# Transformer layer on one core: where sums of w_out, the SSM's preparation and the first transposes stand in the engines' order

## The chip, the cores and the metric

The kernel runs on one core of one Trainium2 chip. The metric is the time of one execution on the device in microseconds (us), lower is better.

## What is computed

One layer of a decoder, in fp32, for one sequence of T = 1024 tokens with D = 1024 (from the reference):

```
x <- LN1(alpha*x + 1/2 * SwiGLU_1(x))                      first FFN ("f1"), FF = 2816
[z_a | z_u | z_v | g_a | g_b] = x @ W_in                   one combined input projection
y_a = S5(z_a) -> GLU -> @ U_a                              diagonal complex SSM branch (causal scan)
y_b = gMLP chunked causal spatial gating(z_u, z_v) -> @ U_b
x <- LN2(alpha*x + (sig(g_a)*y_a + sig(g_b)*y_b) @ W_out)
x <- LN3(alpha*x + 1/2 * SwiGLU_2(x))                      second FFN ("f2")
x <- x + sig(x @ W_pg) * (p @ W_pp)

SwiGLU(x): h = x @ w_in; gate, up = split(h); (silu(gate) * up) @ w_out
```

## The kernel before

Every fp32 product runs on TensorE (PE) as three fp32r matmuls (hi*hi, hi*lo, lo*hi). `split` (L81, L82) makes the two parts: ScalarE (ACT) casts the high part, VectorE (DVE) subtracts it for the low part.

**FFN, into the hidden layer.** `hidden` goes over 22 chunks of 128 hidden columns with gate and up together, by Strassen's scheme in Winograd's form: 7 products per chunk (`prod`, 12 matmuls each) instead of 8. The operands from x are seven blocks, B11, B21, B22, T1 to T4; those from the weights are made per chunk by `pair_steps`: sums s12 and s34 (L312 to L318, DVE), then four splits, named wha/wla, whs/wls, wht/wlt, wh4/wl4 in the trace. The products land in PSUM banks and are read into e0 to e3 by ACT copies (L595, L597, L599, L606) and DVE additions (L603, L608, L610), with ACT's Silu (L604, L609) and the gate (L612, L617) between them. The trace prints e0 to e3 as e_f. ACT and DVE run their instructions in one order each, so L606 stands behind L604, which needs L603. After an odd chunk, `total` (L576) makes sums of two chunks' G, and `put` (L573) stores them from the POOL queue.

**FFN, out of it.** This is Strassen's scheme too, and needs differences of rows of w_out. For each of 11 pairs in each FFN a job "wload" (L256) fetches two blocks of rows of 512 KB on SP's queue, and a job "wsum" (L248) makes four subtracts of 128x512 on DVE and two stores (L250) on POOL's queue. The tiles come from the pool that `phase["rows"]` names: five buffers with tag "s", which s12 and s34 use too, in the first FFN; three buffers with tag "y" in the second. Raw weights have three buffers, split ones five.

**Pre jobs.** At chunks 8 and 14 of the first FFN, jobs "pre" make the split weights of the second FFN's first two chunks and store them; they are loaded back at its start (L241).

**Start.** `x_T` (L763 to L768) transposes a block of x on PE into a transpose bank (`tbank`, two of them) and splits it into xc. Fourteen of these steps are the `feed` of the first chunk, which runs as two halves (columns 0 to 256 and the rest) of seven products: one step ahead of the loop, then one before each product. In the first half a step is x_T of block 1 and a step of the weights' preparation; in the second, x_T of blocks 2 and 3. `turn_vecs` (L365, vecs_t) transposes the vectors of the layer, through the same kind of bank.

**SSM.** `xg_T` (L931 to L936) transposes z_a on PE and copies it, alternately on DVE and ACT, into xg. Then 8 slices follow: each prepares rotation powers (the "e-chain" on DVE, seven levels of L1397 to L1402 behind a copy L1459, and products on POOL and ACT), runs `states` (with a scan) and `outputs` (L1505, matmuls that read ssm_h). `defer(us, ...)` puts a step off by so much estimated PE time.

**Who sets the order.** PE's order is written by hand. On DVE, ACT, POOL and SP a scheduler sets it, except at the very start, where it is the order of the text. `tc.issue_after(i)` obliges it to put instructions behind i on the same engine, without a wait on a semaphore. The first instructions of an SSM slice are put behind the instructions recorded in `last` in this way.

Of the kernel before, what the change touches and what calls it, by code (L numbers as in the profile page):

```python
# [13 lines left out]
ALU = mybir.AluOpType  # L14
# [3 lines left out]
P = 128  # L18
# [12 lines left out]
NCK = T // QS  # L31
# [27 lines left out]
def hybrid_layer(ctx, tc, t, out):  # L59
    nc = tc.nc  # L60
# [157 lines left out]
                i += n  # L218
            g_loaded[ji] = g

    n_made, on_chip, w_rows = [0], {}, {}

    def make_jobs(upto, loading=True):
        while n_made[0] <= min(upto, len(jobs) - 1):
# [6 lines left out]
            if kind in ("pair", "pre"):  # L231
                bs = pair_tiles(i, phase["pre" if kind == "pre" else "pair"][1])
                if raws:
                    for _ in pair_steps(i, loaded[li], loaded[li + 1], bs):
                        pass
                for b, d in zip(bs, pre_d[key[-1]] if kind == "pre" or not raws else ()):
                    for x in range(2):
                        if kind == "pre":
                            nc.gpsimd.dma_start(out=d[x], in_=b[x].bitcast(F32))
                        else:  # L240
                            nc.sync.dma_start(out=b[x].bitcast(F32), in_=d[x])  # L241
                made[key] = pair_views(bs)
            elif kind == "wsum":

                ws = w_rows.pop(key[::2])
                (b11, b12), (b21, b22) = ((r[:, :512], r[:, 512:]) for r in ws)
                for o, x, y in ((b11, b12, b11), (b12, b22, b12), (b22, b22, b11), (b21, b21, b22)):
                    DVE.tensor_tensor(out=o, in0=x, in1=y, op=ALU.subtract)  # L248
                for y in range(2):
                    nc.gpsimd.dma_start(out=wt_d[key[0]][key[2]][y], in_=ws[y])  # L250
            elif kind == "wload":
                p, tag = phase["rows"]
                ws = w_rows[key[::2]] = [p.tile([P, 1024], F32, name=f"wo_{key[0]}_{key[2]}_{y}", tag=tag) for y in range(2)]
                for y in range(2):
                    f = 2 * key[2] + y
                    nc.sync.dma_start(out=ws[y], in_={"f1": w1o, "f2": w2o}[key[0]][f * P:(f + 1) * P, :])  # L256
            else:
                for j in range(i, min(i + RAWBUFS, len(jobs))):
                    load_g(j)
                w, (o_nm, f) = None, (key[0], key[-1])  # L260
                if raws or kind == "out" and order_of(key).index(f) >= WBUFS:
                    w = (wsp_p.tile([P, 1024], F32R, name=f"wh{i}", tag="hi"),
                         wsp_p.tile([P, 1024], F32R, name=f"wl{i}", tag="lo"))
                    on_chip[o_nm, f] = w
                made[key] = on_chip[o_nm, f]
                if raws:
                    split(*w, loaded[li])
                    if o_nm == "mo":
                        for x in range(2):
                            nc.gpsimd.dma_start(out=mo_d[f][x], in_=w[x].bitcast(F32))  # L270
                elif w:
                    for x in range(2):
                        nc.sync.dma_start(out=w[x].bitcast(F32), in_=mo_d[f][x])
                if kind == "out":
                    load_g(i)
                    g, ph = g_loaded.pop(i), phase[key[0]]
                    gh = ph["ghl"].tile([P, 3 * P], F32R, name=f"gh{i}", tag="gh")
                    gl = ph["ghl"].tile([P, 3 * P], F32R, name=f"gl{i}", tag="gl")
                    n = len(ph["sweeps"][key[2]]) * P
                    split(gh[:, :n], gl[:, :n], g[:, :n])  # L280
                    made[key] += (gh, gl)
# [277 lines left out]
    def hidden(nm, xc, g_d, ep, cut, feed=()):  # L559
# [3 lines left out]


        feed = list(feed)
        if feed:
            feed.pop(0)()
        for f, cs in [(0, slice(0, cut)), (0, slice(cut, HT))] + [(f, slice(0, HT)) for f in range(1, NF)]:
            if cs.start == 0:
                w, es = take((nm, "h", f), 0), [ep.tile([P, HT], F32, name=f"e{b}_{nm}_{f}", tag=f"e{b}",  # L570
# [2 lines left out]
                nc.gpsimd.dma_start(out=g_d[f // 2][x], in_=g)  # L573

            def total(x, o, a, b, op):
                DVE.tensor_tensor(out=o, in0=a, in1=b, op=op)  # L576
                put(x, o)

            b1, b2, b3 = (bank(f"p{b}_{nm}_{f}_{cs.start}") for b in range(3))
# [156 lines left out]
    with pool("xc1", side="right") as xc_p, ExitStack() as hs:  # L736
# [23 lines left out]
                    "T3": t13[:, hi], "T4": t24[:, hi]}, todo  # L760

        def x_T(j, name):
            tb, src = tbank(f"xt_x0_{j}_{name}"), blocks[j][name]  # L763
            for i in range(4):
                PE.transpose(tb[:, i * P:(i + 1) * P], src[:, i * P:(i + 1) * P], ident)
            cs = slice(j * P, (j + 1) * P)
# [6 lines left out]
        use = ("B11", "T1", "T2", "B21", "T3", "B22", "T4")  # L773
        for tt in (0, 4):
            load_x(tt)
        load_raws(1)
        for tt in (1, 5):
            load_x(tt)
        rows = load_vecs(ep)
        warm = const.tile([P, 1], F32, name="warm")  # L780
        ACT.activation(out=warm, in_=ident[:, 0:1], func=AF.Silu)
# [87 lines left out]
    with ExitStack() as mx:  # L869
# [62 lines left out]
        def xg_T(q):  # L932
            tb = tbank(f"xg_{q}")
            for i in range(4):
                PE.transpose(tb[:, i * P:(i + 1) * P], za[:, 4 * q + i, :, :].rearrange("p s i -> p (s i)"), ident)
            (ACT.copy if q % 2 else DVE.tensor_copy)(out=xg[:, 4 * q:4 * q + 4, :], in_=tb.rearrange("p (g c) -> p g c", c=NCK))  # L936

        for q in range(NG // 4):
            defer(3.0 + 1.3 * q, ("xg", q), lambda q=q: xg_T(q))
# [429 lines left out]
def ssm_slices(nc, sp, bank, tbank, par, ident, xg, y, defer, need):  # L1369
# [18 lines left out]
    for sl in range(NG // SG):  # L1388
# [80 lines left out]
        def states(sl=sl, t0=t0, tmp=tmp, e=e, er=er, ei=ei, x1=x1, x2=x2):  # L1469
# [23 lines left out]
            for ri, (p1, p2, op) in enumerate(((fr, fi, ALU.subtract), (fi, fr, ALU.add))):  # L1493
                DVE.tensor_tensor(out=y1, in0=gr, in1=p1, op=ALU.mult)
                DVE.tensor_tensor(out=y2, in0=gi, in1=p2, op=ALU.mult)
                for a in range(2):
                    hp = slice(a * NS, (a + 1) * NS)
                    DVE.tensor_tensor(out=hm[ri * NS:(ri + 1) * NS, :, a, 1:P], in0=y1[hp], in1=y2[hp], op=op)
            defer(10.0, ("ssm", sl), lambda: outputs(hm))

        def outputs(hm, sl=sl):
            py = bank(f"ssm_y_{sl}")
# [40 lines left out]
```

## Time and profile before

| | |
|---|---|
| median of 3 runs | 2087.19 us (2085.76 to 2092.68) |
| the profiled execution | 2087.66 us |
| its span, first to last instruction | 2086.0 us |
| mean granted clock of PE | 0.987 |
| PE busy | 2023.9 us, 97% |
| DVE, ACT, POOL busy | 64%, 38%, 14% |
| weight loads of the FFNs (L202) | 88 of 512 KB, median 4.5 us to landing |
| loads of w_out rows (L256) | 44 of 512 KB, median 5.2 us |

An engine's share is over the whole span; the costs of a reordering are read from the stretch in which it works. A granted clock of 1.00 is 2.4 GHz; the other level is 1.2 GHz, and a stretch's figure is a mean.

### The profile page before, as it was taken

The page shows a single profiled execution, that of the slowest core. Times are in us where ns is not written, and L with a number is a line of the kernel's source. Part 1 is how long each engine was busy: PE and PEld are TensorE (multiplying, and loading weights), DVE is VectorE, ACT ScalarE, POOL GpSimd, SP SyncE. Part 2 cuts the span into 40 slices and gives each one's busy share as a digit, 9 for nine tenths or more (in the row PEclk, how much of TensorE's full clock was granted, in tenths as well). Part 3 has the DMA queues.
Part 4 walks back from the last instruction along what each step waited for, and adds up shares of the span by engine and source line. Part 5 has one row for each costly group of instructions (what it writes and reads, how often), then busy time and mean ns, then how long its engine had stood idle before and what let it go on. Part 6 is the DMA issues. An engine that isn't in the chain of part 4 may idle for free.

```text
span 2086.0 us, 25640 instructions
## 1 busy us (share of the span) xinstructions
PE 2023.9 (97%) x9207; PEld 1673.7 (80%) x9207; DVE 1342.8 (64%) x2385; ACT 784.1 (38%) x1227; POOL 282.2 (14%) x443
## 2 busy tenths in 40 slices
PE   7999999999999998999999999889999999999999
PEld 7887878888888896788888788667888888788887
DVE  6767657668557673699544458666665655766852
ACT  4333333333335512334541136223333333334540
POOL 3102111110000132334021200111010010000000
PEclk9999999999999999999999999999999999999999
DMA  4537465547666461222316967883233236766411
GB/s 152 178 127 263 149 220 180 191 121 260 214 196 219 137 198 58 73 82 72 98 60 230 303 234 272 287 277 126 86 111 106 92 116 213 245 196 202 148 61 41
DMA packets 241887, 344.01 MB, mean 165 GB/s; under 512 B 21940, under 2 KB 145936, under 8 KB 241760
## 3 DMA queue, kind: packets, MB, share of 16 engines
q1 hardware_dynamic: 203248, 221.43, 33.7%
q0 software_dynamic: 31600, 108.37, 14.3%
q10 hardware_dynamic: 6912, 12.59, 1.6%
q8 instruction: 72, 1.18, 0.2%
q14 instruction: 55, 0.45, 0.1%
HBM read 232.60 MB, written 108.53 MB: 164 GB/s over the span
## 4 chain that ended last, share of the span: by engine, by line
PE 56%; issue 26%; DVE 7%; DMA 6%; POOL 3%; ACT 1%; SPq 0%; POOLq 0%; DVEq 0%; ACTq 0%
PE po_f L699 19%; PE p_f L555 15%; PE ppg L516 1%; PE ppg L517 1%; PE ppg L518 1%; DMA wo_f<-in_ffn_w_out_dram 1%; POOL g_f_S L573 1%; PE pgb L516 1%; PE pgb L517 1%; PE pgb L518 1%; PE po_mo L516 1%; PE pga L516 1%; PE po_mo L518 1%; PE po_mo L517 1%; PE pga L518 1%
## 5 line engine op out<-in xcount | busy, mean ns | idle before, releaser
L82 DVE TENSOR_TENSOR wl<-wr,wh 128x1024 fp32r<-128x1024 f32 (+1 forms) x254 | 288.0, 1140 | 193.9 <-ACT wh L81 177.6
L81 ACT CAST wh<-wr 128x1024 fp32r<-128x1024 f32 (+1 forms) x254 | 246.7, 978 | 433.3 <-PE po_f L699 153.5
L699 PE MATMUL po_f<-wh 128*128 128x512 f32 x616 | 243.1, 395 | 4.2 <-DVE xa L705 4.2
L699 PE MATMUL po_f<-wh,wl 128*128 128x512 f32 x616 | 241.0, 391 | 0.0
L699 PE MATMUL po_f<-wl,wh 128*128 128x512 f32 x616 | 240.9, 391 | 0.0
L699 PEld LDWEIGHTS po_f<-wh 128*128 128x128 f32 x616 | 116.4, 189 | 28.2 <-issue 4.5
L699 PEld LDWEIGHTS po_f<-wh,wl 128*128 128x128 f32 x616 | 116.3, 189 | 24.7
L699 PEld LDWEIGHTS po_f<-wl,wh 128*128 128x128 f32 x616 | 116.5, 189 | 23.6
L573 POOL DMA_DIRECT2D g_f_A<-e_f x66 | 36.0, 545 | 540.1 <-DVE e_f L612 273.8
L312 DVE TENSOR_TENSOR s<-wr 128x512 f32<-128x512 f32 x44 | 30.9, 702 | 119.6 <-DMA wr<-in_ffn_w_in_dram 119.6
L555 PE MATMUL p_f<-T4h,wh 128*128 128x512 f32 (+3 forms) x184 | 74.7, 406 | 15.1 <-ACT e_f L606 15.1
L555 PE MATMUL p_f<-T2h,whs 128*128 128x512 f32 (+3 forms) x184 | 72.0, 391 | 6.9 <-ACT e_f L595 6.9
L81 ACT CAST whs<-s 128x1024 fp32r<-128x1024 f32 x44 | 46.2, 1050 | 81.5 <-PE p_f L555 60.5
L555 PE MATMUL p_f<-T3h,wht 128*128 128x512 f32 (+3 forms) x184 | 72.2, 392 | 4.5 <-ACT e_f L599 4.5
L555 PE MATMUL p_f<-T4l,wh 128*128 128x512 f32 (+3 forms) x184 | 73.7, 400 | 0.4 <-DVE T4l L82 0.4
L555 PE MATMUL p_f<-T4h,wl 128*128 128x512 f32 (+3 forms) x184 | 73.5, 399 | 0.0
L555 PE MATMUL p_f<-T3l,wht 128*128 128x512 f32 (+3 forms) x184 | 71.3, 387 | 1.9 <-DVE T3l L82 1.9
L82 DVE TENSOR_TENSOR wlt<-s,wht 128x1024 fp32r<-128x1024 f32 x44 | 53.8, 1223 | 29.6 <-ACT wht L81 26.8
L81 ACT CAST wht<-s 128x1024 fp32r<-128x1024 f32 x44 | 46.2, 1049 | 70.9 <-PE p_f L555 70.6
L555 PE MATMUL p_f<-B11l,wha 128*128 128x512 f32 (+3 forms) x184 | 70.6, 384 | 1.7 <-DVE B11l L82 1.7
L555 PE MATMUL p_f<-T1h,whs 128*128 128x512 f32 (+3 forms) x184 | 71.0, 386 | 0.9 <-ACT whs L81 0.9
L555 PE MATMUL p_f<-T1h,wls 128*128 128x512 f32 (+3 forms) x184 | 70.9, 385 | 0.8 <-DVE wls L82 0.8
(391 smaller groups left out, 5225.6 us busy)
## 6 DMA issues: line engine op xcount, KB each, us to landing
wr<-in_ffn_w_in_dram SPq DMA_DIRECT2D x88, 512.0 KB, 4.5
wo_f<-in_ffn_w_out_dram SPq DMA_DIRECT2D x44, 512.0 KB, 5.2
wt_f<-wo_f POOLq DMA_DIRECT2D x44, 512.0 KB, 4.3
wr<-wt_f SPq DMA_DIRECT2D x88, 256.0 KB, 3.3
wr<-g_f_S SPq DMA_DIRECT2D x88, 256.0 KB, 3.7
g_f_A<-e_f POOLq DMA_DIRECT2D x66, 256.0 KB, 3.0
g_f_S<-g_f POOLq DMA_DIRECT2D x66, 256.0 KB, 4.4
wr<-in_ffn_w_out_dram SPq DMA_DIRECT2D x66, 256.0 KB, 3.5
```

Source lines behind the costliest of these rows:

```text
L81: ACT.copy(out=hi, in_=src)
L82: DVE.tensor_sub(out=lo, in0=src, in1=hi.bitcast(F32))
L312: DVE.tensor_tensor(out=s1, in0=a21, in1=a22, op=ALU.add)
L516: PE.matmul(acc, lhsT=ah, rhs=bh, start=start, stop=False)
L517: PE.matmul(acc, lhsT=ah, rhs=bl, start=False, stop=False)
L518: PE.matmul(acc, lhsT=al, rhs=bh, start=False, stop=stop)
L555: PE.matmul(acc[:, cs], lhsT=p, rhs=q, start=start and k == 0 and i == 0, stop=stop and k == HK - 1 and i == 2, skip_group_check=True)
L573: nc.gpsimd.dma_start(out=g_d[f // 2][x], in_=g)
L699: PE.matmul(acc[t], lhsT=a[:, c], rhs=b[:, :512], start=not more and i == 0 and k == 0, stop=i == NP - 1 and k == 2, skip_group_check=True)
```

## The change

Nothing is computed otherwise. (1) The four subtracts of a "wsum" are put behind the last `total` made so far on DVE, the two loads of a "wload" behind the last weight load on SP. (2) Two steps of the feed run ahead of the first chunk's loop instead of one. (3) Block 3's transposes use the product banks (`bank`, six) instead of the transpose banks. (4) x blocks 1 and 5 are loaded before the first weights. (5) The copies to xg are recorded in `last[0]` and `last[1]`, so that the preparation of the first slice stands behind them on DVE and ACT. (6) A slice's outputs are put off by 12.5 instead of 10.0.

```diff
-    n_made, on_chip, w_rows = [0], {}, {}
+    n_made, on_chip, w_rows, last_sum = [0], {}, {}, [None]
...
-                for o, x, y in ((b11, b12, b11), (b12, b22, b12), (b22, b22, b11), (b21, b21, b22)):
-                    DVE.tensor_tensor(out=o, in0=x, in1=y, op=ALU.subtract)
+                with tc.issue_after(last_sum[0].ins):
+                    for o, x, y in ((b11, b12, b11), (b12, b22, b12), (b22, b22, b11), (b21, b21, b22)):
+                        DVE.tensor_tensor(out=o, in0=x, in1=y, op=ALU.subtract)
...
-                for y in range(2):
-                    f = 2 * key[2] + y
-                    nc.sync.dma_start(out=ws[y], in_={"f1": w1o, "f2": w2o}[key[0]][f * P:(f + 1) * P, :])
+                with tc.issue_after(last_load[0].ins):
+                    for y in range(2):
+                        f = 2 * key[2] + y
+                        nc.sync.dma_start(out=ws[y], in_={"f1": w1o, "f2": w2o}[key[0]][f * P:(f + 1) * P, :])
...
-        if feed:
-            feed.pop(0)()
+        for fn in feed[:2]:
+            fn()
+        feed = feed[2:]
...
-                DVE.tensor_tensor(out=o, in0=a, in1=b, op=op)
+                last_sum[0] = DVE.tensor_tensor(out=o, in0=a, in1=b, op=op)
...
-            tb, src = tbank(f"xt_x0_{j}_{name}"), blocks[j][name]
+            tb, src = (bank if j == 3 else tbank)(f"xt_x0_{j}_{name}"), blocks[j][name]
...
-        load_raws(1)
         for tt in (1, 5):
             load_x(tt)
+        load_raws(1)
...
-            (ACT.copy if q % 2 else DVE.tensor_copy)(out=xg[:, 4 * q:4 * q + 4, :], in_=tb.rearrange("p (g c) -> p g c", c=NCK))
+            last[q % 2] = (ACT.copy if q % 2 else DVE.tensor_copy)(out=xg[:, 4 * q:4 * q + 4, :], in_=tb.rearrange("p (g c) -> p g c", c=NCK))
...
-            defer(10.0, ("ssm", sl), lambda: outputs(hm))
+            defer(12.5, ("ssm", sl), lambda: outputs(hm))
```

The line numbers of the rows below are those of the kernel they are taken from; the changed kernel's are one to three higher (L248 is L249, L256 is L258, L576 is L579, L603 is L606, L936 is L939).

DVE in chunk 1 of the second FFN, before. wo_f2_2_1 is the second row block of w_out's pair 2, wlt188 and wla190 are split weights, e0_f2_1 is chunk 1's e0:

```order
L248 TENSOR_TENSOR wo_f2_2_1_11838<-wo_f2_2_1_11838 128x512
L248 TENSOR_TENSOR wo_f2_3_0_12116<-wo_f2_3_0_12116 128x512
L82 TENSOR_TENSOR wlt188_11288<-s34_188_11292,wht188_11287 128x1024
L248 TENSOR_TENSOR wo_f2_3_0_12116<-wo_f2_3_1_12117,wo_f2_3_0_12116 128x512
L603 TENSOR_TENSOR e0_f2_1_11272<-e0_f2_1_11272,p1_f2_1_0_11277 128x512
```

And after the change, from the last sums of G of chunk 1 to L606 (the former L603) of chunk 2:

```order
L579 TENSOR_TENSOR g_f2_1_11410<-e0_f2_1_11272,g_f2_0_11269 128x512
L249 TENSOR_TENSOR wo_f2_0_0_11279<-wo_f2_0_0_11279 128x512
L249 TENSOR_TENSOR wo_f2_0_0_11279<-wo_f2_0_1_11280,wo_f2_0_0_11279 128x512
L249 TENSOR_TENSOR wo_f2_0_1_11280<-wo_f2_0_1_11280,wo_f2_0_0_11279 128x512
L314 TENSOR_TENSOR s12_192_11570<-wr176_11448 128x512
L249 TENSOR_TENSOR wo_f2_0_1_11280<-wo_f2_0_1_11280 128x512
L315 TENSOR_TENSOR s12_192_11570<-s12_192_11570,wr175_11307 128x512
L319 TENSOR_TENSOR s34_192_11571<-wr175_11307,wr176_11448 128x512
L320 TENSOR_TENSOR s34_192_11571<-wr175_11307,s12_192_11570 128x512
L82 TENSOR_TENSOR wlt190_11431<-s34_190_11435,wht190_11430 128x1024
L606 TENSOR_TENSOR e0_f2_2_11413<-e0_f2_2_11413,p1_f2_2_0_11418 128x512
```

Before, pair 3's subtracts stood ahead of chunk 1's L603; now pair 0's stand behind chunk 1's sums of G, with no subtract of a later pair before chunk 3's end.

SP's queue at the start of the second FFN, before:

```order
L256 DMA wo_f2_1_1_11559<-in_ffn2_w_out_dram 128x1024
L256 DMA wo_f2_2_0_11837<-in_ffn2_w_out_dram 128x1024
L202 DMA wr174_11305<-in_ffn2_w_in_dram 128x8x128
L256 DMA wo_f2_2_1_11838<-in_ffn2_w_out_dram 128x1024
L241 DMA wh4_186_11163<-pre1_3_0_286 128x512
L241 DMA wl4_186_11164<-pre1_3_1_287 128x512
L256 DMA wo_f2_3_0_12116<-in_ffn2_w_out_dram 128x1024
L256 DMA wo_f2_3_1_12117<-in_ffn2_w_out_dram 128x1024
L256 DMA wo_f2_4_0_12395<-in_ffn2_w_out_dram 128x1024
L202 DMA wr175_11307<-in_ffn2_w_in_dram 128x8x128
```

And after the change:

```order
L202 DMA wr174_11305<-in_ffn2_w_in_dram 128x8x128
L241 DMA wh4_186_11163<-pre1_3_0_286 128x512
L241 DMA wl4_186_11164<-pre1_3_1_287 128x512
L202 DMA wr175_11307<-in_ffn2_w_in_dram 128x8x128
L202 DMA wr176_11448<-in_ffn2_w_in_dram 128x8x128
L202 DMA wr177_11450<-in_ffn2_w_in_dram 128x8x128
L258 DMA wo_f2_1_0_11558<-in_ffn2_w_out_dram 128x1024
L258 DMA wo_f2_1_1_11559<-in_ffn2_w_out_dram 128x1024
L202 DMA wr178_11584<-in_ffn2_w_in_dram 128x8x128
```

The loads of w_out rows (wo) stood between the first weight loads (wr); now one pair's two follow four weight loads.

DVE at xg, after the change (before, all of the e-chain stood ahead of the first copy to xg):

```order
L82 TENSOR_TENSOR wl135_6626<-wr137_6381,wh135_6625 128x1024
L939 COPY xg_6617<-xg_0_6670 128x512
L939 COPY xg_6617<-xg_2_6694 128x512
L939 COPY xg_6617<-xg_4_6735 128x512
L939 COPY xg_6617<-xg_6_6759 128x512
L1462 COPY ssm_e_0_7014<-par_rot_4462 128x2 x2
L1400 TENSOR_TENSOR ssm_x1_0_7015<-ssm_e_0_7014,par_rot_4462 128x2
```

The copies have moved ahead of the whole e-chain, which begins with L1462.

## Rows read from the trace of the kernel before

**Rows 1.** The head of the page and its part 1, whole span
```profile
span 2086.0 us, 25640 instructions
PE 2023.9 (97%) x9207; PEld 1673.7 (80%) x9207; DVE 1342.8 (64%) x2385; ACT 784.1 (38%) x1227; POOL 282.2 (14%) x443
```

**Rows 2.** Table by stretches: stretch, its length, busy us (instructions) per engine, PEclk, DMA share, GB/s
```profile
18.00:60.00 42.00, 33.60 (x249) 31.83 (x247) 32.70 (x48) 21.84 (x40) 11.12 (x8) 0.92 0.21 65
60.00:100.00 40.00, 40.00 (x176) 32.69 (x175) 30.83 (x45) 15.72 (x22) 6.35 (x12) 1.00 0.57 191
160.00:200.00 40.00, 36.92 (x160) 29.50 (x159) 26.88 (x38) 16.89 (x24) 7.43 (x14) 1.00 0.76 262
280.00:320.00 40.00, 35.40 (x145) 28.07 (x145) 25.56 (x35) 15.34 (x22) 7.51 (x14) 0.96 0.77 258
780.00:820.00 40.00, 31.26 (x146) 26.68 (x146) 21.32 (x54) 9.80 (x20) 10.76 (x17) 0.87 0.29 87
820.00:840.00 20.00, 20.00 (x90) 16.57 (x89) 2.45 (x2) 4.51 (x6) 0.00 (x0) 1.00 0.14 40
920.00:940.00 20.00, 18.17 (x84) 15.21 (x83) 18.76 (x67) 6.25 (x13) 5.07 (x8) 0.91 0.20 61
1300.00:1420.00 120.00, 100.83 (x433) 81.35 (x432) 80.03 (x121) 33.24 (x52) 20.52 (x38) 0.91 0.77 263
1420.00:1460.00 40.00, 40.00 (x176) 32.75 (x175) 22.96 (x30) 14.28 (x21) 3.80 (x7) 1.00 0.35 110
```

**Rows 3.** Waits of DVE, ACT and PE from 1295 to 1420: total us, times, longest
```profile
DVE wo_f L248 <- DMA wo_f<-in_ffn_w_out_dram: 32.6, 11, 6.4
ACT e_f L604 <- DVE e_f L603: 30.3, 5, 8.2
PE p_f L555 <- ACT e_f L606: 15.1, 5, 4.6
PE p_f L555 <- ACT e_f L595: 3.7, 2, 3.3
```

**Rows 4.** Timeline of DVE and PE: start, us, then line and operation, [idle before]
```profile
1334.06 0.69 DVE L248 TENSOR_TENSOR wo_f<-wo_f,wo_f 128x512 f32<-128x512 f32 x1 [3.26 <-DMA wo_f<-in_ffn_w_out_dram]
...
1334.67 0.68 DVE L603 TENSOR_TENSOR e_f<-e_f,p_f 128x512 f32<-128x512 f32 x1
...
1336.54 0.74 PE L555 MATMUL p_f<-T4h,wh 128*128 128x512 f32 x1 [4.55 <-ACT e_f L606]
```

**Rows 5.** The subtracts of L248 over the span: ns min/median/max
```profile
L248 DVE TENSOR_TENSOR wo_f<-wo_f x44: 647/684/694, 64.2 to 1411.6; 128x512 f32<-128x512 f32 x44
```

**Rows 6.** DVE in steady chunks: timeline (second FFN), waits from 60 to 140 (first)
```profile
1460.43 0.69 DVE L312 TENSOR_TENSOR s<-wr 128x512 f32<-128x512 f32 x1 [4.20 <-DMA wr<-in_ffn_w_in_dram]
DVE s L312 <- DMA wr<-in_ffn_w_in_dram: 13.5, 4, 4.7
```

**Rows 7.** Waits of DVE from 160 to 200
```profile
DVE s L312 <- DMA wr<-in_ffn_w_in_dram: 8.4, 2, 4.8
DVE wls L82 <- DMA pre<-wlt: 4.0, 1, 4.0
```

**Rows 8.** Timeline of DVE and PE around z_a, and the e-chain's next reader
```profile
786.46 0.24 DVE L1459 COPY ssm_e<-par_rot 128x2 f32<-128x2 f32 x2 [2.64 <-DMA x_d<-g]
...
802.34 0.68 DVE L936 COPY xg<-xg 128x512 f32<-128x512 f32 x1
...
803.08 1.12 PE L935 MATMUL xg<-ident,za 128*128 128x128 f32 x4 [8.50 <-DVE xg L936]
...
858.92 0.80 DVE L1397 TENSOR_TENSOR ssm_x<-ssm_bs,ssm_e 128x256 f32<-128x256 f32 x1 [3.62 <-ACT ssm_bs L1479]
```

**Rows 9.** Waits of PE from 18 to 60
```profile
PE vecs_t L365 <- issue: 2.1, 1, 2.1
PE p_f L555 <- DVE T3l L82: 1.9, 1, 1.9
```

**Rows 10.** Waits of PE from 900 to 980
```profile
PE ssm_y L1505 <- DVE ssm_h L1498: 2.7, 2, 1.8
```

## The prediction, written before the changed kernel was run

> **What bounds the kernel.** I read the page first. TensorE (PE) is busy for 2023.9 of a span of 2086.0 us [rows 1], so all that a reordering can give back is the 62.1 us in which PE stands still, and what it loses at a lower clock around them. No other engine is near its limit over the whole span (VectorE, DVE, 64%). So the second view is the table by stretches [rows 2]: it shows where PE loses time, and which clock it was granted. In most of the span it loses nothing: between 60 and 100 us, and between 1420 and 1460, PE is busy for 40.00 of 40 us at clock 1.00. The losses lie in five places, and an edit is aimed at each. Idle is the stretch minus PE's busy time; the clock's part is at most (1 - clock) times the stretch, at most because some of the low-clock time lies in the idle itself:
> - start, 18 to 60: idle 8.4, clock up to 3.4
> - two "pre" chunks, 160 to 200 and 280 to 320: idle 3.1 and 4.6, clock up to 1.6
> - z_a, 780 to 820: idle 8.7, clock up to 5.2
> - SSM slices, 920 to 940: idle 1.8, clock up to 1.8
> - start of the second FFN, 1300 to 1420: idle 19.2, clock up to 10.8
>
> The clock is told by the rows alone: a mean of 0.91 is a mix of its two levels, 2.4 and 1.2 GHz; it stands below 1.00 only in stretches in which PE also stood still, and at 1.00 where PE is fed. A closed gap should therefore take its low-clock time along, and I count a part of it, named at each term. Third come the waits of each engine in those stretches, and the rows in order of time, which say who was late. No instruction is added or removed by the change, on any engine; everything is a matter of order.
>
> **Second FFN, sums and loads of w_out.** The largest loss has a chain of three. DVE waited 32.6 us in 11 waits for w_out rows (L248), ScalarE (ACT) waited 30.3 us in 5 for DVE's L603, and PE waited 15.1 us in 5 for ACT's L606 [rows 3]. In order of time [rows 4]: DVE stands 3.26 us before a subtract at 1334.06, only then does L603 run (1334.67), behind it ACT's L604 and L606, and T4's first matmul starts at 1336.54 after 4.55 us of idle. So eleven pairs of sums stand in DVE's line ahead of e's additions, before their rows have come, because the 22 loads are all pulled forward, with the last subtract at 1411.6 [rows 5], a quarter into this FFN's 22 chunks; the DMA share is 0.77 there and 0.35 behind [rows 2]. The change puts each pair's four subtracts behind the G sums of an odd chunk, so that L603 has none of them ahead of it that still waits for a load, and puts its loads behind the weight loads, one pair in two chunks. What goes: the 15.1 us for L606, and the waits for L595 (3.7), whose ACT queue stands behind L609 that waits for DVE in the same way: some 18.5 of the 19.2 us of idle. Of the clock's 10.8 I count six tenths, 6.5, as part of the slow stretch is idle already. Term **-25**, between -18 (idle alone) and -30 (everything).
>
> What the moved work costs where it now stands: four subtracts of 0.684 us [rows 5] are 2.7 us on DVE per odd chunk, 11 of them in each FFN, 60 us of DVE in all. It had this work already (in the first FFN from 64.2 on), and a chunk takes some 19.6 us on PE (7 products of 12 matmuls at 0.233). DVE is busy 30.8 of 40 in the first FFN with sums in it and 23.0 of 40 in the second without [rows 2], so 9 and 17 us in two chunks are free. Right where the sums now stand, before the next pair's s12 and s34 (L312 to L318), DVE waits for weights anyway: 4.20 us at 1460.43, 13.5 us in 4 waits in the first FFN, 3.4 each [rows 6]. 2.7 is less than 3.4, so I cost them at 0; without that cover L603 of an even chunk would be late by up to 2.7. On SP's queue two loads now stand between weight loads, waiting for a free tile (three in the second FFN), which the store behind the last pair's sums frees. The weight load behind them waits for the last read of an older weight block, later in the same chunk, so I see no delay; bounds 0 and the mean wait of today, 32.6/11 = 3.0 us a pair. On POOL's queue the two stores stand behind the G stores and have 20 us. The DMAs' bytes stay the same. The trace speaks for holding these loads back: the early ones are what stands in the way. The Trainium skill's DMA: Bandwidth & Descriptors (section Rules for kernel authors) says the opposite in general: issue a DMA early, compute, and wait late. By it the term would be nothing or a loss; the row at 1334.06 differs, in that there the consumer's place in DVE's line came early with the load.
>
> **Pre chunks.** In 160 to 200, L312 waited 8.4 us in 2 for weights and a split 4.0 for the pre store [rows 7]; L248 sums and two wo loads stand ahead of that pair's work. After the change sums stand elsewhere and wo loads behind the chunk's weights. The pair's loads come by some microseconds earlier, but two pairs' weights and their stores still run in one chunk. Idle 7.7 and clock 1.6 are the end, 0 the other; I take just over half, **-5**.
>
> **z_a.** PE stands 8.50 us until 803.08 for xg's copy on DVE, which runs at 802.34 since DVE worked through the e-chain (and two splits) from 786.46 [rows 8]. The change puts the copies of xg first and the chain behind them. The transposes' matmuls then wait for nothing but one copy of 0.68, beside which PE has other products. The idle goes, and of the clock's 5.2 the 2.2 that lie behind 803: **-10.5**, ends -8 (0.7 left for the copy) and -13.9. The chain's results are next read at 858.92, and between 820 and 840 DVE is busy for 2.45 of 20 [rows 2, 8], so its 15 us fit behind the copies; with no such room they would come back at the first slice.
>
> **Start.** PE's waits there include 2.1 at vecs_t, which uses the two transpose banks, and 1.9 for T3l [rows 9]. x_T two products ahead gives each split one product more (14 half-width products share these 42 us, 3.0 each), block 3's transposes get the six product banks instead of two, and x blocks 1 and 5 load before the weights, at whose cast no wait shows. Against it: one more transpose and split, 0.6 to 0.7, stand before the first product, and DVE is busy for 32.7 of 42 us [rows 2], which cannot be pressed far. I take 2.1 + 1.9 and some 2 of what remains and of the clock: **-6**, between +0.7 and -11.8.
>
> **Slices.** PE waited 2.7 us in 2 for ssm_h [rows 10]; outputs 2.5 us later (12.5 for 10.0) covers this, with 1.8 of clock at most: **-3**. DVE is busy 18.76 of 20 us there, so a later output may make something else late: +1 to -4.5.
>
> **Sum.** -25 - 5 - 10.5 - 6 - 3 = -49.5. The profiled execution took 2087.66 us (span 2086.0 and 1.66 around it), 0.47 over the median of the runs, so the sums agree with either: 2087.66 - 49.5 = **2038 us**.
>
> **Rivals.**
> (a) The sums come back as a wait, slower. Held back to the chunk's end, with rows that land late, the four subtracts push L603 of the next chunk, as they do today in the second FFN, once in each odd chunk of both FFNs. By their own length it is 22 x 2.7 = 60 us: 2038 + 60 = 2098. It decides from the point at which a chunk's DVE work passes its free time, 4.5 us per chunk in the first FFN, so from 1.8 us of waiting beside the 2.7 on. For it: tiles are few (five "s" tiles shared with s12 and s34, three "y" tiles), and a load waits for one. Against it: the free time, and the wait for weights just there. 5%. The Trainium skill's rule named above would lead here.
> (b) The second FFN's stall is DMA load. The share is 0.77, and late weights would remain: the first chunks stay slow, 2038 + 25 = 2063. Against it: the bytes now spread over 430 us. 10%.
> (c) Start and pre chunks give nothing, since DVE or the pair's stores are the limit: 2038 + 11 = 2049. 15%.
> (d) Everything closes, ends of all terms: -30 - 9.3 - 13.9 - 11.8 - 4.5 = -69.5, 2018. Rather a bound; 2030 and less 10%.
> (e) The order does not do it: the scheduler or a new wait right behind each gap takes it all, 2087. 4%.
>
> **Chances and range.** The forecast has 56%. A measurement of this kernel can tell about 0.3%, 6.3 us, from no change. Faster by more: forecast, (b), (c), (d), 91%; within: (e), 4%; slower: (a), 5%. The range goes from 2022, near (d), to 2064, which takes in (b); outside are (a), (e) and half of (d)'s edge.
>
> **What would show it.** Right: between 1300 and 1420 PE busy near 118 of 120 us at a clock near 0.99, no L606 wait, DMA share near 0.5 there and higher than 0.35 behind; no wait before xg, with DVE's e-chain behind the copies; 160 to 200 and 280 to 320 with half their idle; vecs_t's wait gone. Wrong: DVE waits for wo_f at the end of odd chunks and PE's idle spread by 20 us steps through both FFNs; weights (wr) late behind wo loads on SP; a wait for ssm_h or ssm_e before a slice's output.

## The result, and the profile after

The changed kernel takes 2041.99 us (median of 4 runs, 2039.88 to 2045.26) against 2088.81 us for the kernel before on the same chip: a ratio of 0.9774 (95% interval 0.9753 to 0.9795). The forecast was 2038, the range 2022 to 2064. The profiled execution took 2040.58 us with a span of 2038.9, that is 47.1 us less of span than before. PE is busy for 2012.3 of it: its idle time fell from 62.1 to 26.6 us.

The head of the changed kernel's page and its part 1:

```profile
span 2038.9 us, 25680 instructions
PE 2012.3 (99%) x9207; PEld 1666.8 (82%) x9207; DVE 1344.1 (66%) x2385; ACT 782.9 (38%) x1225; POOL 282.1 (14%) x443
```

The table by stretches, columns as in [rows 2]. All stages start earlier now, so the stretches of z_a and of the second FFN are shifted to hold the same work (12 and 27 us earlier):

```profile
18.00:60.00 42.00, 35.62 (x265) 33.55 (x266) 36.87 (x51) 21.67 (x41) 13.11 (x10) 0.96 0.18 52
160.00:200.00 40.00, 40.00 (x174) 32.39 (x173) 30.47 (x41) 17.18 (x24) 9.05 (x17) 1.00 0.78 264
280.00:320.00 40.00, 40.00 (x175) 32.44 (x174) 29.33 (x39) 17.90 (x24) 8.05 (x15) 1.00 0.77 263
768.00:808.00 40.00, 39.76 (x193) 34.07 (x193) 16.28 (x54) 12.73 (x25) 12.17 (x17) 1.00 0.31 98
1273.00:1393.00 120.00, 119.09 (x536) 99.10 (x536) 76.44 (x110) 42.12 (x64) 14.38 (x27) 0.96 0.43 146
1393.00:1433.00 40.00, 40.00 (x174) 32.55 (x173) 26.54 (x36) 14.89 (x21) 5.09 (x10) 1.00 0.47 159
```

Against [rows 2]: the pre chunks and z_a have no idle left but 0.24 us, at a clock of 1.00 instead of 0.87 to 1.00. The second FFN's start has 0.9 us of idle instead of 19.2. Behind it the DMA share went up from 0.35 to 0.47, as the loads and stores of w_out rows now fill all of this FFN.

The waits of the stretch that lost most (DVE, ACT and PE from 1269 to 1393), which answer to [rows 3]:

```profile
DVE s L314 <- DMA wr<-in_ffn_w_in_dram: 15.2, 6, 4.1
...
ACT e_f L607 <- DVE e_f L606: 0.5, 1, 0.5
...
PE p_f L557 <- DVE T2l L82: 0.5, 1, 0.5
PE p_f L557 <- ACT e_f L598: 0.4, 1, 0.4
PE p_f L557 <- ACT e_f L609: 0.2, 1, 0.2
```

No subtract of w_out rows waits there any more (32.6 us in 11 before). ACT's wait for DVE's addition fell from 30.3 us to 0.5, and PE's wait for the copy behind it (L606, now L609) from 15.1 to 0.2. What DVE waits for now is weights, 15.2 us in 6, and PE does not feel it.

The queues' own view shows what the trace of before had held beside that. SP's waits at the second FFN's start, before (1290 to 1420) and then after (1265 to 1400):

```profile
SPq L256 <- DMA wt_f<-wo_f: 73.9, 18, 7.4
```

```profile
SPq L202 <- DVE wla L82: 73.1, 7, 13.6
SPq L202 <- DVE wl L82: 32.8, 5, 7.1
```

Before, SP stood for 73.9 of 130 us with a load of w_out rows at its head, waiting until a store freed one of the three tiles. After, it waits for the last read of a weight buffer, as in the steady chunks.

To see where the 47.1 us came from, I took the start of the first matmul of each stage in PE's timeline in both traces:

| stage (from, to) | us before | forecast | measured |
|---|---|---|---|
| start, to chunk 1 | 59.88 | -6 | -4.45 |
| pre chunks, where the jobs of chunks 8 and 14 are made | 49.09 | -5 | -9.98 |
| last chunks of the first FFN, 18 to 21 | 77.77 | 0 | +3.31 |
| z_a and z_u, to the g_a products | 114.48 | -10.5 | -10.82 |
| SSM slices | 329.82 | -3 | -1.98 |
| second FFN, chunks 0 to 4 | 134.31 | -25 | -24.07 |
| second FFN, chunks 5 to 21 | 327.76 | 0 | +2.93 |
| all the rest | 992.84 | 0 | -2.03 |
| sum | 2085.95 | -49.5 | -47.09 |

The -24.07 is +2.89 in chunk 0 and -26.96 in chunks 1 to 4. (Two of the expectations quoted below, those of the sums and loads together and of the whole start, count the two halves of chunk 0 as two chunks: their chunk 2 is chunk 1 here, and their 19 to 22 are 18 to 21.)

### The profile page after: what moved, and what is told of

It reads as the page before. It is cut to its first block, busy times and chain, and to the rows that moved or that the text cites. A ratio compares the mean times of both kernels' runs of the same rounds, so it can differ in the third digit from the quotient of the medians.

```text
span 2038.9 us, 25680 instructions
## 1 busy us (share of the span) xinstructions
PE 2012.3 (99%) x9207; PEld 1666.8 (82%) x9207; DVE 1344.1 (66%) x2385; ACT 782.9 (38%) x1225; POOL 282.1 (14%) x443
## 4 chain that ended last, share of the span: by engine, by line
PE 51%; issue 34%; DVE 6%; POOL 5%; DMA 1%; ACT 1%; POOLq 0%; SPq 0%; DVEq 0%; ACTq 0%
PE po_f L702 19%; PE p_f L557 3%; POOL g_f_S L576 2%; POOL g_f_A L576 2%; PE ppg L519 1%; PE ppg L518 1%; PE ppg L520 1%; PE po_mo L518 1%; PE po_mo L519 1%; PE po_mo L520 1%; POOL wt_f L251 1%; PE pga L518 1%; PE pgb L518 1%; PE pga L520 1%; PE pgb L520 1%
## 5 line engine op out<-in xcount | busy, mean ns | idle before, releaser
L576 POOL DMA_DIRECT2D g_f_A<-e_f x66 | 35.8, 543 | 636.4 <-DVE e_f L615 366.6
L557 PE MATMUL p_f<-B22l,wht 128*128 128x512 f32 (+3 forms) x184 | 71.5, 388 | 0.4 <-DVE B22l L82 0.4
L557 PE MATMUL p_f<-B22h,wlt 128*128 128x512 f32 (+3 forms) x184 | 71.6, 389 | 0.0
L557 PE MATMUL p_f<-T3h,wlt 128*128 128x512 f32 (+3 forms) x184 | 71.6, 389 | 0.0
L557 PE MATMUL p_f<-B11h,wha 128*128 128x512 f32 (+3 forms) x184 | 71.5, 389 | 0.0
L557 PE MATMUL p_f<-T2l,whs 128*128 128x512 f32 (+3 forms) x184 | 70.9, 385 | 0.5 <-DVE T2l L82 0.5
```

Source lines behind the costliest of these rows:

```text
L557: PE.matmul(acc[:, cs], lhsT=p, rhs=q, start=start and k == 0 and i == 0, stop=stop and k == HK - 1 and i == 2, skip_group_check=True)
```

## The experiments

Each run below was made from one of the two kernels. Their stages were read in the same way as in the table. Where a stage of a run holds the same instructions in the same order as before, its length still differed by a few us from execution to execution, against the one trace of before: at the pre chunks by -4.8 to +4.9 us in the four runs on the kernel before that left sums and loads alone, in chunk 0 of the second FFN by +0.2 to +6.3 in those four, in its chunks 1 to 4 by -5.3 to +2.2 (where chunk 0 was long they were short; together +0.5 to +2.5), and at the start by -0.8 to +1.9 in the four that left the start alone. The five traces with all edits of the start on the changed kernel gained 4.5 to 7.6 there. A single stage speaks only beyond that.

### Is it the place of the sums, the loads, or both?

Edit (1) alone on the kernel before, both halves:

```diff
+                with tc.issue_after(last_sum[0].ins):
                     for o, x, y in ((b11, b12, b11), (b12, b22, b12), (b22, b22, b11), (b21, b21, b22)):
                         DVE.tensor_tensor(out=o, in0=x, in1=y, op=ALU.subtract)
...
+                with tc.issue_after(last_load[0].ins):
                     for y in range(2):
```

> The kernel before with edit (1) alone: the four subtracts of a pair behind the last sums of G on DVE, the two loads behind the last weight load on SP. My theory, that the second FFN's start and the pre chunks lose their time to the place of these instructions and to nothing else: the span falls by the same as the changed kernel's does in these two stretches, 24 us at the second FFN's start and 10 in the two pre chunks, less 3 for the new waits in chunks 19 to 22 of the first FFN and 3 for a slower pace of the second FFN's later chunks: about 2086.0 - 28 = 2058 us of span; z_a, the start and the slices lose what they lost before. Rival, that the pre chunks were helped by the earlier start (edits 2 to 4 shift what meets what in the DMA queues): 24 - 6 = 18 us, 2068.

Measured: 2061.25 us, ratio 0.9868 (0.9848 to 0.9888), span 2062.8. Chunks 1 to 4 of the second FFN gained 27.1 us, the pre chunks 8.9, the last chunks of the first FFN lost 3.3: the same as in the full change, to 1.1 us. So the pre chunks' gain is edit (1)'s, and so is the new loss at the end of the first FFN; the rival with the earlier start falls. That the span is 4.8 us above the 2058 expected comes most of all from chunk 0 of the second FFN (+4.6) and the start (+1.9), within the scatter.

Then the subtracts alone held back, with the loads as before:

> The kernel before with the subtracts alone held back, the loads free. Theory, that the subtracts' place in DVE's line is the cause: the second FFN's start gains the full 24 us, since L603 no longer stands behind a subtract that waits, and the loads are throttled by the three tiles anyway. Rival, that the early loads are the cause (SP's queue and DMA load): a load that is early in SP's queue now waits there for a tile that comes free only behind an odd chunk, with weight loads behind it, and the stretch gains less than 10 us or loses.

Measured: 2059.89 us, ratio 0.9863 (0.984 to 0.9887). And the loads alone, with the subtracts free:

> The kernel before with the loads alone held back behind the weight loads, the subtracts free. Theory, that a subtract ahead of L603 costs only where its rows have not landed: with two loads in two chunks at most four subtracts stand in two chunks, and they can be placed anywhere; the scheduler puts none ahead of L603 of a chunk whose rows are late, so the start of the second FFN gains most of the 24 us (18 or more). Rival, that both edits are needed: under 12 us. The pre chunks show which of the two edits their 10 us belong to: by the theory (loads of w_out ahead of the chunk's weights) this run has them and the one with the subtracts alone has less.

Measured: 2065.59 us, ratio 0.9889 (0.9865 to 0.9914). The stretch of 120 us at the second FFN's start, in the table by stretches, with the subtracts held:

```profile
1290.00:1410.00 120.00, 118.94 (x546) 100.49 (x545) 73.36 (x106) 48.42 (x80) 10.83 (x20) 0.94 0.43 143
```

and with the loads held:

```profile
1290.00:1410.00 120.00, 118.92 (x542) 100.38 (x541) 75.41 (x108) 47.56 (x79) 11.88 (x22) 0.94 0.43 145
```

Either half alone brings the whole gain there: -26.2 and -26.8 us in chunks 1 to 4 against -27.1 with both. Both theories had forecast the gain, each from a cause of its own; but the two are not separate causes, they hold each other. Three tiles tie them into a ring: a load waits for a tile, the tile for the store, the store for the subtract, the subtract for the load. Slow down one of these and all of them follow. The traces show it: counted from this FFN's first matmul, the last pair's loads are issued from 116 us on before, but from 374 on with the subtracts alone held back; the last pair's subtracts begin at 122 us before, but at 386 with the loads alone held back. The rival for the run with the subtracts alone (early loads then block SP's queue) did occur, but small: SP waits 19.6 us for tiles, 73.9 before, with no loss on PE.

The two halves differ in the first FFN. With the subtracts held alone, the first sum of s12 (L313 there) waits for tiles on DVE in six places; the rows are of DVE's waits from 60 to 470 us:

```profile
DVE s L313 <- DMA wr<-in_ffn_w_in_dram: 40.3, 12, 7.1
DVE s L313 <- DMA wt_f<-wo_f: 32.2, 6, 6.4
```

Chunks 8 to 12 lost 3.5 us by it, and the pre chunks gained 6.0, little beyond the scatter. With the loads held alone they gained 0.7, which is within it. In all six runs with both halves the pre chunks are 8.9 to 10.1 us shorter, so they want both. The expectation had this the other way round, with the 10 us in the run with the loads held.

### Is the second FFN's start a matter of DMA load?

The changed kernel, with copies that nothing waits for:

```diff
             load_raws(li + len(raws) - 1)
+            if kind == "pair" and key[0] == "f2" and 2 <= key[2] <= 6:
+                with tc.issue_after(last_load[0].ins):
+                    for y in range(3):
+                        f = 3 * (key[2] - 2) + y
+                        nc.sync.dma_start(out=dram.tile([P, D], F32, name=f"junk{f}"), in_=w2o[f * P:(f + 1) * P, :])
             if kind in ("pair", "pre"):
```

> The changed kernel with 15 more copies of 512 KB from w_out to a scratch tensor in DRAM, which nothing waits for, three behind the weight loads of each of five chunks at the start of the second FFN: they bring the DMA load of that stretch back to about what it was before (each reads and writes 512 KB, as a load and a store of rows do). Theory, that the stall came from DVE's line: PE loses nothing by them there, under 3 us, with the DMA share near 0.8. Rival, that the stall was DMA load: most of the 24 us come back, as waits for weights (s on wr) or for what hangs on them.

Measured: 2043.34 us, ratio 0.9777 (0.9758 to 0.9796), against 0.9774 for the change. The same 120 us as above:

```profile
1273.00:1393.00 120.00, 119.09 (x536) 99.73 (x535) 75.42 (x108) 43.17 (x66) 13.89 (x26) 0.94 0.54 189
```

PE is busy for 119.09 us, to the digit what it is without the copies. They raised the DMA share from 0.43 to 0.54 only, not to the 0.77 of before, so the test covers a third of the way. Three of the 15 copies were issued at 1182 to 1187 us already, ahead of the stretch. Where the others begin, the share is 0.63, for 0.45 without them, and PE loses nothing:

```profile
1300.00:1340.00 40.00, 40.00 (x176) 32.75 (x175) 24.63 (x33) 15.19 (x22) 4.88 (x9) 1.00 0.63 230
```

The two runs above don't help against this rival, as the DMA share fell to 0.43 in both as well. Two other readings do. In the kernel before, late weights, by which the rival would act, were a small part of DVE's waits from 1295 to 1420, next to the 32.6 us for w_out rows:

```profile
DVE s L312 <- DMA wr<-in_ffn_w_in_dram: 4.0, 3, 2.6
```

And the pre chunk of the changed kernel has a DMA share of 0.78 with PE busy for 40.00 of 40 us. So the rival of DMA load has no support left, though it wasn't tested in this stretch at the 0.77 of before.

### z_a

Edit (5) alone on the kernel before:

```diff
-            (ACT.copy if q % 2 else DVE.tensor_copy)(out=xg[:, 4 * q:4 * q + 4, :], in_=tb.rearrange("p (g c) -> p g c", c=NCK))
+            last[q % 2] = (ACT.copy if q % 2 else DVE.tensor_copy)(out=xg[:, 4 * q:4 * q + 4, :], in_=tb.rearrange("p (g c) -> p g c", c=NCK))
```

> The kernel before with edit (5) alone: the copies to xg recorded, the first slice's preparation behind them. Theory: the gap of 8.5 us before xg and the low clock behind it go, nothing else changes: 2086.0 - 10.8 = 2075 us of span. Rival, that the e-chain comes back as a wait of the first slices: 5 us or less gained.

Measured: 2075.10 us, ratio 0.9939 (0.9916 to 0.9961), span 2074.6. The stage is 10.82 us shorter, as in the full change, and the slices did not change (-0.2), against the rival, that the e-chain comes back as a wait there. The same stretch as in [rows 2]:

```profile
780.00:820.00 40.00, 39.76 (x195) 33.46 (x195) 14.87 (x53) 13.26 (x25) 11.44 (x17) 1.00 0.24 70
```

31.26 became 39.76 of 40 at a clock of 1.00 for 0.87. The first copy runs as soon as its transposes are done, and the e-chain begins behind the fourth, DVE's timeline of this run:

```profile
788.19 0.69 DVE L936 COPY xg<-xg 128x512 f32<-128x512 f32 x1 [0.54 <-PE xg L935]
...
800.40 0.69 DVE L936 COPY xg<-xg 128x512 f32<-128x512 f32 x1 [2.96 <-PE xg L935]
801.01 0.23 DVE L1459 COPY ssm_e<-par_rot 128x2 f32<-128x2 f32 x2
```

### The start

Edits (2), (3) and (4) together; then (2) alone; then (3) and (4) without (2), all on the kernel before:

```diff
-        if feed:
-            feed.pop(0)()
+        for fn in feed[:2]:
+            fn()
+        feed = feed[2:]
```

```diff
-            tb, src = tbank(f"xt_x0_{j}_{name}"), blocks[j][name]
+            tb, src = (bank if j == 3 else tbank)(f"xt_x0_{j}_{name}"), blocks[j][name]
...
-        load_raws(1)
         for tt in (1, 5):
             load_x(tt)
+        load_raws(1)
```

> The kernel before with edits (2), (3) and (4) alone, those of the start. Theory: chunk 2 begins 4.5 us earlier, as in the changed kernel, and nothing else changes: some 2081.5 us of span, give or take the 3 us that a low-clock stretch more or less makes in one execution. Rival, that the start gained from the held sums and loads (they first stand in chunks 1 and 2): under 2 us.

> The kernel before with edit (2) alone: two steps of the feed ahead of the loop, the transposes of block 3 still in the two transpose banks, the weights loaded first. Theory, as the prediction has it, that being a product ahead is what closes the gaps and the banks give 2.1 us at vecs_t: half of the 4.5 us here. Rival, that the transpose banks are the limit (a transpose two products ahead needs a bank that an earlier split still holds): no gain at all, or slower, and edit (3) is what pays.

> The kernel before with edits (3) and (4) alone: block 3's transposes in the product banks, x blocks 1 and 5 loaded ahead of the weights, one step of the feed ahead of the loop as before. Since edit (2) alone made the start 4.5 us longer, and all three make it 4 us shorter: if the transpose banks are the limit and the step ahead is worth something only with enough of them, this run gains under 2 us at the start; if the banks alone pay, it gains 4 us or more.

Measured: all three 2083.46 us, ratio 0.9976 (0.9962 to 0.999), chunk 1 begins 3.95 us earlier. The step ahead alone 2093.02 us, ratio 1.0022 (1.0004 to 1.004): a little slower, chunk 1 begins 4.45 us later (in a profiled execution that was the longest of ten, 2103.59 us). The banks and the order of the loads alone 2087.99 us, ratio 0.9995 (0.9978 to 1.0011): no change, chunk 1 begins 0.28 us later. PE's waits from 15 to 70 us with the step ahead alone, and then, from 17 to 70, with the banks alone:

```profile
PE xt_x_B L766 <- issue: 3.8, 1, 3.8
PE vecs_t L365 <- issue: 3.0, 1, 3.0
PE xt_x_T L766 <- DVE B11l L82: 1.8, 1, 1.8
```

```profile
PE p_f L555 <- DVE T3l L82: 4.7, 2, 2.4
PE p_f L555 <- ACT whs L81: 2.3, 1, 2.3
PE p_f L555 <- DVE B11l L82: 1.0, 1, 1.0
```

With the step ahead alone the rival came true (slower), but the banks alone don't pay either. One step further ahead, two transposes wait at PE for 3.8 and 3.0 us, and the products behind them in PE's order wait with them. Of the 4.45 us, 3.2 lie ahead of the first product already, where two transposes wait 1.4 and 1.8 us for a split (before, PE waits 1.7 us for the second of these splits inside that product). The profile names no releaser ("issue"); both use the two transpose banks, and both waits are gone where block 3 has the product banks, so a bank that an earlier split still holds is the likely one. With more banks but no step ahead, the wait at vecs_t is gone, and the products wait for the splits, T3l 4.7 us. Only both together help: in the run with all three neither row is left, and what remains are transposes that wait up to 1.8 us each for a split. The run with (3) and (4) doesn't part these two from each other, but what (4) does can be read: before, DVE waits 1.05 us for the second pair of x blocks to land (1.58 with the step ahead alone), and this wait is gone in both runs with (4).

### The slices

The changed kernel with `defer(10.0, ...)` in place of `defer(12.5, ...)`:

> The changed kernel with the slices' outputs put off by 10.0 again (edit (6) undone). Theory, as the prediction has it (3 us): the slices take 2 us longer and PE's wait for ssm_h is longer than the 2.9 us it has in the changed kernel. Rival, that the 2 us came from elsewhere (the slices' DVE work is at its limit, and a later output only moves the wait): no difference beyond 0.5 us.

Measured: 2043.35 us, ratio 0.9774 (0.975 to 0.9798), the ratio of the change itself. The times can't tell the theory's 2 us, or the prediction's 3, from the rival of nothing. In the traces the slices are 3.3 us longer than with 12.5; 1.7 of them are a stretch of low clock behind the longer wait. PE's wait, from 840 to 1160, with 10.0 and then with 12.5:

```profile
PE ssm_y L1508 <- DVE ssm_h L1501: 3.6, 2, 1.8
```

```profile
PE ssm_y L1508 <- DVE ssm_h L1501: 2.9, 4, 1.5
```

The single wait became shorter, and there are more of them. Taken over all traces the sum of this wait didn't change: 2.6 to 3.6 us in the nine with 10.0 (the kernel before among them), 2.7 to 3.6 in the four with 12.5. DVE is busy for 94.59 of 100 us there (860 to 960), so a later output gives it little. The stage did become shorter all the same: it takes 329.0 to 331.2 us in those nine and 327.5 to 328.3 in those four, some 2 us less, in two ranges that don't meet. With 10.0 a stretch of 3.4 us at the lower clock, worth 1.7, lies in seven of the nine; with 12.5 it lies in none.

### A version that beats both

From chunk 18 on the changed kernel has a new wait. DVE's waits from 380 to 470, a row of DVE's timeline, and PE's waits from 360 to 470:

```profile
DVE s L319 <- DMA wt_f<-wo_f: 10.1, 2, 5.6
```

```profile
397.52 0.69 DVE L319 TENSOR_TENSOR s<-wr,wr 128x512 f32<-128x512 f32 x1 [5.55 <-DMA wt_f<-wo_f]
```

```profile
PE p_f L557 <- ACT e_f L609: 2.8, 3, 1.1
```

Pairs 8, 10 and 9 follow each other in three consecutive chunks, as pair 10's job was put at chunk 20. Their tiles and those of s12 and s34 share five buffers, and s34 waits until a store has freed one. I left the number of buffers as it is and moved one job:

```diff
-        sums = {f: (f - 3) // 2 if f % 2 else NP - 1 for f in (*range(3, NF, 2), NF - 2)}
+        sums = {f: (f - 3) // 2 if f % 2 else NP - 1 for f in (2, *range(3, NF, 2))}
```

> The changed kernel with pair 10 of w_out's rows, whose job stands at chunk 20, moved to chunk 2 in both FFNs, so that no three pairs follow in consecutive chunks at the end (19, 20, 21). Theory: the new waits of the changed kernel, s34 on a tile that the last pair's store holds (10.1 us in 2 waits on DVE, 3.0 us on PE), stand there because 4 tiles of rows and 2 of sums want 5 buffers; with a pair in every second chunk alone they go, and the first FFN ends 3 us earlier. Rival, that they come back at chunks 2 and 3, where two pairs now follow each other: no gain, 1 to 3 us lost there.

Measured: 2037.53 us, ratio 0.9754 (0.974 to 0.9769). Its interval overlaps that of the change, so the times alone don't part the two; in the trace the +3.3 us are gone (0.00), and PE has no wait at all from 360 to 470. Where two pairs now follow each other, from 55 to 130, s34 waits 2.2 us for a tile, and PE is busy for 40.00 of 40 us from 55 to 95. The start of this execution was also 3.1 us shorter than the changed kernel's, which the edit doesn't touch and the scatter covers.

The second gap that was left stood in both kernels: at the end of the second FFN's first output product PE waits 4.2 and 4.3 us for L708's addition to x (L705 before), which stands behind the preparation of x's block 7. With the job moved as above, and in addition:

```diff
-Y_AT = {2: 4, 3: 5, 5: 6, 7: 7, 9: 0, 13: 1, 15: 2, 17: 3}
+Y_AT = {2: 4, 3: 5, 4: 6, 5: 7, 11: 0, 13: 1, 15: 2, 17: 3}
```

> The changed kernel with pair 10's job at chunk 2, as in the run before, and the loads of x's blocks for the output of an FFN moved: blocks 6 and 7 one and two steps earlier, block 0 two steps later, behind the end of the first product. Theory: the wait of 4.3 us on xa at the start of the second FFN's output (3.3 in the run before) stands because block 7 lands late and its two DVE operations come last before it; it goes with part of the low-clock stretch behind it, 4 to 6 us: some 2032 us. Rival, that the loads crowd the weights there (DMA share 0.8): the wait moves to a split, no gain.

Measured: 2031.74 us, ratio 0.9718 (0.9693 to 0.9742), the fastest version here, 10 us under the change. PE's waits from 1690 to 1760:

```profile
PE po_f L702 <- DVE wl L82: 0.6, 1, 0.6
PE po_f L702 <- DVE xa L708: 0.5, 1, 0.5
```

Of the 4.3 us 1.1 are left, 0.6 of them in a split, where the rival had the whole wait go.

## Why the prediction was right, and where it was not

**Second FFN (-25, measured -24.07): right.** The waits along the chain DVE, ACT, PE went as a whole, with 18.3 of 19.2 us of idle. Of the clock's 10.8 us about 6 came back, for the 6.5 counted. The cover that the sums were costed at nothing with held: DVE's sums of a pair now stand where it would wait for weights (at L314 it waits 0.59 and 2.20 us in two chunks with sums, 3.82 and 4.12 in two without), PE is busy for 40.00 of 40 us behind, and rival (a), 2.7 us in each odd chunk of both FFNs, didn't occur there. Three things were off. The cause is not the subtracts' place alone: the runs with one half of the edit each show a ring of loads, tiles, subtracts and stores that either half breaks. The DMA share fell further than I said, to 0.43 instead of near 0.5. And the clock of the stretch is 0.96 instead of near 0.99, by a stretch of low clock in chunk 0 that its waits don't account for (last section). The Trainium skill's rule in DMA: Bandwidth & Descriptors (section Rules for kernel authors), to issue a DMA early and wait late, would have made this term nothing or a loss. The trace of before shows the other side of it: the loads that were issued early held SP's queue for 73.9 us, as the tile was not free, and the wait that came late stood in front of work that PE needed.

**Pre chunks (-5, measured -9.98): right in kind, mis-sized.** The step that failed is "I take just over half", on the ground that two pairs' weights and their stores still run in one chunk. They do, the DMA share is 0.78 as before (0.76), and PE still lost nothing: 40.00 of 40 in both stretches. DVE's waits from 160 to 200 after the change, which answer to [rows 7]:

```profile
DVE wla L82 <- DMA pre<-wls: 1.8, 1, 1.8
DVE s L314 <- DMA wr<-in_ffn_w_in_dram: 1.8, 1, 1.8
...
DVE wlt L82 <- DMA pre<-wla: 0.6, 1, 0.6
```

12.4 us of waits for DMAs became 4.2. What had made PE wait was the order, not the traffic. The upper bound of 9.3 was the better value.

**z_a (-10.5, measured -10.82): right** to 0.3 us, and the run with this edit alone gave the same. The terms that it names come to a little more than it says: 8.5 of idle (8.7 in the list of losses) and 2.2 of clock are 10.7 (10.9).

**Start (-6, measured -4.45 here, -6.0 to -7.6 in four other runs on the changed kernel, and -3.95 with the same edits on the kernel before): the size right, the ground half wrong.** "x_T two products ahead gives each split one product more" was to pay by itself; alone it made the kernel a little slower; it paid only together with the banks and the order of the loads. The 2.1 at vecs_t is gone, the 1.9 for T3l as well, but transposes now wait for splits: DVE is busy for 36.9 of 42 us instead of 32.7, the limit that the prediction named.

**Slices (-3, measured -1.98 in this trace): the size near, the ground wrong.** The step that failed is "outputs 2.5 us later (12.5 for 10.0) covers this": the wait for ssm_h is 2.9 us in 4 after, 2.7 in 2 before. It is one of the signs of being wrong that the prediction named. What went is a stretch of low clock behind it, which the prediction counted with 1.8 us at most.

**What the sum left out.** The new wait in chunks 18 to 21 (+3.3) is like rival (a) in a corner, with s34 that waits for a tile in place of the sums: the tiles were too few exactly where three pairs follow each other. The prediction had "tiles are few" in its rival, and took the pairs to be evenly spread, one in two chunks; the job list has one at chunk 20. The table of jobs would have shown it. The later chunks of the second FFN (+2.9) are no cost of the change, see below. Together, 6.2, they outweigh what the pre chunks gave beyond the forecast, 5.0. That the whole came within 2.4 us of the forecast, -47.09 for -49.5, is in part luck: these errors nearly cancel.

## What to carry to other kernels

When a queue that runs in order holds an instruction whose data come from far, its place is a cost to everything behind it; put it where that engine would wait anyway, and count what shares its buffers. In a ring of load, tile, work and store, holding back one member held back all here, so look for the cheapest one to hold. Being further ahead paid only with buffers to be ahead in: test such edits together as well as apart.

## What the runs showed of the hardware beside that

The e-chain of z_a took 14.8 us before (786.46 to 801.3, with a split of 1.65 in it) and 8.4 us behind the copies (792.53 to 800.95). The same product of 128x4 in DVE's timeline, before, while POOL worked on products of its own, and after, while POOL stood idle:

```profile
788.47 0.71 DVE L1398 TENSOR_TENSOR ssm_x<-ssm_e,par_rot 128x4 f32<-128x4 f32 x1
```

```profile
793.74 0.15 DVE L1401 TENSOR_TENSOR ssm_x<-ssm_e,par_rot 128x4 f32<-128x4 f32 x1
```

POOL's products take 0.62 us, about what the DVE instruction lost (0.56). After, the one operation of the chain that starts while POOL works (128x32, at 796.89) takes 0.50 us; its twin at 797.75 takes 0.19. This agrees with the Trainium skill, SBUF — State Buffer (section Who interferes with whom), by which a DVE operation with two inputs from SBUF and a GpSimd operation that reads SBUF take turns on a shared port pair. Nothing in the sum hung on it, since the chain is off the path now.

The pace of PE in the chunks differs by 1.6% (19.28 or 19.59 us a chunk) with nothing to show for it: twelve matmuls of 512 columns take 2.75 or 2.80 us, for whole chunks at a time, with no idle and a clock of 1.00. Before, all the later chunks of the second FFN ran at the faster pace; in the changed kernel every second one ran at the slower, 0.31 us a pair, 2.9 us in all. The same came in the run with edit (5) alone, whose second FFN is that of before, and it did not come in the runs with the subtracts alone and with the extra copies. So it doesn't follow the change. Each kernel has one trace, so whether it goes with the execution or with the program is not shown; its cause stays open.

The clock, too, does not follow the waits alone. In the changed kernel the first chunk of the second FFN has waits of 0.5 and 0.4 us, and then a stretch at the lower level (1.2 GHz); in the kernel before PE waited 0.4 and 0.5 us in the same place, and no such stretch follows within the same work. The 16 us from there on, after and then before:

```profile
1276.00:1292.00 16.00, 15.47 (x77) 14.47 (x77) 9.43 (x17) 4.47 (x9) 1.09 (x2) 0.68 0.46 149
```

```profile
1300.00:1316.00 16.00, 14.73 (x101) 12.95 (x99) 9.54 (x18) 4.50 (x10) 1.07 (x2) 1.00 0.54 174
```

Chunk 0 is 2.9 us longer with it. The two waits of 0.4 and 0.5 us stand in this place in all thirteen traces; the low stretch follows in eleven of them, that of edit (5) alone among them, and not in the kernel before and in the run with the edits of the start alone. What decides it was not tried.
